# A dilated convolution on one core: four input buffers, a rearranged head, and stores on the software DMA queue

## The chip, the cores and the metric

The kernel runs on one core of a Trainium2 chip. The metric is the device time of a run in microseconds (us). A profiled execution also has a span, from its first to its last instruction, which is shorter than the measured time by 1.7 to 3.4 us in the runs of this case. Runs are sorted into fast and slow executions. The ratios below use fast ones alone; medians and ranges are over all runs, a few slow ones included. The kept profile of the kernel before is of a run classed slow (134.03 us).

## The reference

Sixteen images of 64 channels and 64x64 pixels are convolved with 128 filters of 3x3 at dilation 2, zero padded, in f32.

```python
def setup_inputs():
    batch, c_in, h, w, c_out, k, dilation = 16, 64, 64, 64, 128, 3, 2
    return {"x": randn(batch, c_in, h, w), "weight": randn(c_out, c_in, k, k) * 0.1, "dilation": dilation}

def reference(x, weight, dilation):
    # ... padding by 2 ...
    for kh in range(k):
        for kw in range(k):          # (loops over b, co, ci left out)
            output[b, co] += weight[co, ci, kh, kw] * x_pad[b, ci, kh*2:kh*2+h, kw*2:kw*2+w]
```

The input has 16.8 MB and the output 33.6 MB. Both are f32, so with 0.3 MB of weights 50.6 MB have to move whatever the kernel does.

## The kernel before

Two images form a pair: 128 partitions of 64x64 values, one load of 2.1 MB. A pair is computed in four groups of 16 output rows, so there are 32 groups. For each group ScalarE casts a chunk of the f32 pair to f16 (`cast`), VectorE adds row pairs (`rowsum`), TensorE makes three products (`psP`, `psA`, `psB`), ScalarE copies `psP` out of PSUM (`p_sb`), and VectorE adds it to `psA` and to `psB` on the way to the output buffer `osb` (`evac`). A finished pair is 4.2 MB, stored in two DMAs of 2.1 MB; only the first and the last pair are stored in halves. The instructions of each engine run in the order written. The parts that the change touches, shortened, with comments added:

```python
    LOOK = 4
    x32pool = ctx.enter_context(tc.tile_pool(name="x32pool", bufs=3))   # f32 pairs, 16 KB a partition
    xpool = ctx.enter_context(tc.tile_pool(name="xpool", bufs=3))       # f16 pairs
    opool = ctx.enter_context(tc.tile_pool(name="opool", bufs=3))       # output pairs, 32 KB a partition
    # ...
    def store(pb, m, lo, hi):
        nc.sync.dma_start(                       # loads are on nc.sync too
            out=out_img[2 * pb + m, :, lo * W : hi * W],
            in_=o_tiles[pb][:, m * HW + lo * W : m * HW + hi * W],
        )

    nc.sync.dma_start(out=w32, in_=weight.rearrange("o i h w -> o (i h w)"))
    first = [[H]] * 3
    for pb in range(min(3, npairs)):
        load(pb, first[pb])
    # ... identity; 14 warm matmuls into an "ab" PSUM tile ...
    # ... weights are combined and cast into wd ...
    cast(0)
    # ...
    rowsum(0)
    # ... wd is transposed on TensorE and copied from PSUM to w_sb by VectorE and ScalarE ...

    ahead = [1, 1]
    def prepare(n):
        n = min(n, ngroups)
        while ahead[1] < min(n - 1 if n < ngroups else n, ahead[0]):
            rowsum(ahead[1]); ahead[1] += 1
        while ahead[0] < n:
            cast(ahead[0]); ahead[0] += 1
    prepare(2)
    freed = [0]

    for G in range(ngroups):
        # ... products psP, psA, psB; copy p_sb ...
        evac(0, psA)
        prepare(min(G + 3 + G // 3, G + 1 + LOOK))
        evac(1, psB)
        if ahead[0] >= NG * (freed[0] + 1) and freed[0] + 3 < npairs:
            load(freed[0] + 3, [H])              # waits until the old pair is cast
            freed[0] += 1
        if pb in (0, npairs - 1) and g % 2 == 1:
            for m in range(2):
                store(pb, m, (g - 1) * GR, (g + 1) * GR)
        elif 0 < pb < npairs - 1 and g == NG - 1:
            for m in range(2):
                store(pb, m, 0, H)
```

Of the kernel before, what the change touches and what calls it, by code (L numbers as in the profile page):

```python
# [10 lines left out]
def kernel(  # L11
# [18 lines left out]
    nc = tc.nc  # L30

    B, CI, H, W = x.shape
# [7 lines left out]
    P = 128  # L40
    f32 = mybir.dt.float32
# [6 lines left out]
    NG = H // GR  # L48
    NBLK = GR // 4
    NH = GR // 2 * W  # L50
    npairs = B // 2
    ngroups = npairs * NG
    chunk_rows = [(g * GR + (d if g else 0), min((g + 1) * GR + d, H)) for g in range(NG)]
    LOOK = 4

    wpool = ctx.enter_context(tc.tile_pool(name="wpool", bufs=1))
    x32pool = ctx.enter_context(tc.tile_pool(name="x32pool", bufs=3))
    xpool = ctx.enter_context(tc.tile_pool(name="xpool", bufs=3))
    opool = ctx.enter_context(tc.tile_pool(name="opool", bufs=3))
    spool = ctx.enter_context(tc.tile_pool(name="spool", bufs=2))  # L60
    ppool = ctx.enter_context(tc.tile_pool(name="ppool", bufs=1, space=bass.MemoryType.PSUM))
    apool = ctx.enter_context(tc.tile_pool(name="apool", bufs=3, space=bass.MemoryType.PSUM))
# [9 lines left out]
    def load(pb, rows):  # L72

        t = x32pool.tile([P, HW], f32, tag="x32", name="x32")
        x32_tiles[pb] = t
        lo = 0
        for hi in rows:
            nc.sync.dma_start(out=t[:, lo * W : hi * W], in_=x_pair[pb, :, lo * W : hi * W])
            lo = hi

    def cast(c):
        pb, g = divmod(c, NG)
        lo, hi = chunk_rows[g]
        if g == 0:
            x16_tiles[pb] = xpool.tile([P, HW], f16, tag="x16", name="x16")
            xs_tiles[pb] = xpool.tile([P, HW // 2], f16, tag="xs", name="xs")
        nc.scalar.copy(  # L87
            out=x16_tiles[pb][:, lo * W : hi * W], in_=x32_tiles[pb][:, lo * W : hi * W]
        )

    def rowsum(c):
        pb, g = divmod(c, NG)
        v = x16_tiles[pb][:, g * GR * W : (g + 1) * GR * W].rearrange(
            "p (b e q) -> p b e q", e=2, q=2 * W
        )
        s = xs_tiles[pb][:, g * NH : (g + 1) * NH].rearrange("p (b q) -> p b q", q=2 * W)
        nc.vector.tensor_tensor(out=s, in0=v[:, :, 0], in1=v[:, :, 1], op=add)  # L97

    def store(pb, m, lo, hi):
        nc.sync.dma_start(  # L100
            out=out_img[2 * pb + m, :, lo * W : hi * W],
            in_=o_tiles[pb][:, m * HW + lo * W : m * HW + hi * W],
        )
# [3 lines left out]

    w32 = wpool.tile([CO, CI * KH * KW], f32, name="w32")
    nc.sync.dma_start(out=w32, in_=weight.rearrange("o i h w -> o (i h w)"))
    first = [[H]] * 3  # L110
    for pb in range(min(3, npairs)):
        load(pb, first[pb])

    ident = wpool.tile([P, P], f16, name="ident")
    make_identity(nc, ident)
# [1 line left out]

    warm = wpool.tile([P, 512], f16, name="warm")
    nc.vector.memset(warm, 0.0)  # L119
    wp = apool.tile([P, 1024], f32, tag="ab", name="wp")  # L120
    for i in range(14):
        nc.tensor.matmul(out=wp[:, 0:512], lhsT=warm[:, 0:P], rhs=warm)  # L122


    KINDS = 5
# [6 lines left out]
    for r in range(2):  # L132
        nc.vector.tensor_tensor(out=wdv[:, 1, :, r], in0=wv[:, 2], in1=wv[:, 1], op=sub)
        nc.scalar.copy(out=wdv[:, 4, :, r], in_=wv[:, 2])
    cast(0)
    for r in range(2):
        nc.vector.tensor_tensor(out=wdv[:, 3, :, r], in0=wv[:, 0], in1=wv[:, 1], op=sub)
    rowsum(0)
    w_sb = wpool.tile([P, KINDS * KW * CO], f16, name="w_sb")
    NT = KINDS * KW  # L140
    for q, n in ((0, 8), (8, 7)):
        wt = apool.tile([P, 1024], f32, tag="ab", name="wt")
        for t in range(q, q + n):
            nc.tensor.matmul(
                out=wt[:, (t - q) * CO : (t - q + 1) * CO],
                lhsT=wd[:, t * 2 * CI : (t + 1) * 2 * CI],
                rhs=ident,
# [5 lines left out]
    def product(ps, src, kind, blk0, nblk, first, last):  # L153

        for j in (1, 0, 2):
            dw = (j - 1) * d
            o0, o1 = max(0, -dw), W - max(0, dw)
            t = kind * KW + j
            for hb in range(2):
                pp = slice(hb * CI, (hb + 1) * CI)  # L160
                rhs = src(pp, dw + o0, dw + o1)
                po = ps[:, hb * NH + blk0 * 2 * W : hb * NH + (blk0 + nblk) * 2 * W]
                po = po.rearrange("p (r w) -> p r w", w=W)[:, :, o0:o1]
                nc.tensor.matmul(  # L164
                    out=po,
                    lhsT=w_sb[pp, t * CO : (t + 1) * CO],
                    rhs=rhs,
                    start=first and j == 1,
                    stop=last and j == 2,
                )  # L170

    def blocks(x16, b0, n, e):

        v = x16.rearrange("p (b e r w) -> p b e r w", e=2, r=2, w=W)
        return lambda pp, c0, c1: v[pp, b0 : b0 + n, e, :, c0:c1]

    ahead = [1, 1]

    def prepare(n):

        n = min(n, ngroups)
        while ahead[1] < min(n - 1 if n < ngroups else n, ahead[0]):
            rowsum(ahead[1])
            ahead[1] += 1
        while ahead[0] < n:
            cast(ahead[0])
            ahead[0] += 1

    prepare(2)
    freed = [0]  # L190

    for G in range(ngroups):
        pb, g = divmod(G, NG)
        x16 = x16_tiles[pb]
        xs = xs_tiles[pb].rearrange("p (r w) -> p r w", w=W)
        if g == 0:
            o_tiles[pb] = opool.tile([P, 2 * HW], f32, tag="osb", name="osb")
        o = o_tiles[pb].rearrange("p (m b e q) -> p m b e q", m=2, e=2, q=2 * W)
        b0 = g * NBLK

        psP = ppool.tile([P, 2 * NH], f32, tag="p", name="psP")
        sv = lambda pp, c0, c1: xs[pp, g * GR // 2 : (g + 1) * GR // 2, c0:c1]
        product(psP, sv, 0, 0, NBLK, True, True)

        psA = apool.tile([P, 2 * NH], f32, tag="ab", name="psA")
        product(psA, blocks(x16, b0, NBLK, 1), 1, 0, NBLK, True, False)
        z = 1 if g == 0 else 0
        product(psA, blocks(x16, b0 + z - 1, NBLK - z, 1), 2, z, NBLK - z, False, True)

        psB = apool.tile([P, 2 * NH], f32, tag="ab", name="psB")  # L210
        product(psB, blocks(x16, b0, NBLK, 0), 3, 0, NBLK, True, False)
        z = 1 if g == NG - 1 else 0
        product(psB, blocks(x16, b0 + 1, NBLK - z, 0), 4, 0, NBLK - z, False, True)

        p_sb = spool.tile([P, 2 * NH], f32, tag="psb", name="p_sb")
        nc.scalar.copy(out=p_sb, in_=psP)  # L216
        pv = p_sb.rearrange("p (m b q) -> p m b q", m=2, q=2 * W)

        def evac(e, ps):
            nc.vector.tensor_tensor(  # L220
                out=o[:, :, b0 : b0 + NBLK, e],
                in0=ps.rearrange("p (m b q) -> p m b q", m=2, q=2 * W),
                in1=pv,
                op=add,
            )

        evac(0, psA)
        prepare(min(G + 3 + G // 3, G + 1 + LOOK))
        evac(1, psB)

        if ahead[0] >= NG * (freed[0] + 1) and freed[0] + 3 < npairs:
            load(freed[0] + 3, [H])
            freed[0] += 1
        if pb in (0, npairs - 1) and g % 2 == 1:
            for m in range(2):
# [4 lines that stand above are left out]
# [35 lines left out]
```

## Time and profile before

| | before |
|---|---|
| measured, first three runs | 133.54 us median (132.32 to 134.15) |
| span of the profiled run | 131.3 us |
| bytes moved | 50.76 MB, mean 387 GB/s |
| rate when nothing disturbs (50 to 100 us) | 429 GB/s |
| PE busy | 107.2 us (82%) |
| end of the last evacuation | 116.6 us |

The page of the kernel before, its head. The rows with digits cut the span into 40 slices of 3.28 us; a digit is the busy share of a slice in tenths. DMA is the mean share of the 16 DMA engines and GB/s what they moved.

```profile
span 131.3 us, 2313 instructions
...
PE   6906898888999999999999999999999999900000
...
DMA  5999938999999999999999999999999999999960
GB/s 165 399 424 439 424 160 274 359 397 419 429 432 334 369 299 434 424 412 444 424 439 424 422 429 429 434 429 419 429 434 434 414 434 429 429 419 417 429 284 17
DMA packets 4185, 50.76 MB, mean 387 GB/s; under 512 B 464, under 2 KB 464, under 8 KB 592
...
```

PE looks like the bottleneck for two thirds of the span, but its row ends in zeros: TensorE is done at 115, and the DMA row goes on. 50.76 MB at 429 GB/s need 118 us, so the transfers bound the kernel, and what matters is where the GB/s row is low after the first slice: slices 5 to 8 and 12 to 14, counted from 0, that is about 16 to 30 and 39 to 49 us.

The same in stages (table by stage of the kernel before). The first numbers of a row are the stretch and its length, then the busy time of each engine with its instruction count, and the last three are the granted TensorE clock, the share of the DMA engines, and GB/s.

```profile
...
core 0: us, PE busy (x) PEld busy (x) DVE busy (x) ACT busy (x) POOL busy (x), PEclk, DMA share, GB/s
3.00:16.00 13.00, 8.61 (x56) 3.71 (x54) 5.01 (x11) 6.88 (x10) 0.00 (x0) 0.87 0.98 415
16.00:30.00 14.00, 12.05 (x112) 5.22 (x114) 9.71 (x13) 8.10 (x9) 0.00 (x0) 1.00 0.82 305
30.00:50.00 20.00, 19.54 (x190) 8.99 (x188) 17.39 (x21) 13.36 (x14) 0.00 (x0) 1.00 0.98 382
50.00:100.00 50.00, 50.00 (x488) 23.65 (x486) 43.59 (x50) 31.32 (x32) 0.00 (x0) 1.00 1.01 429
100.00:118.00 18.00, 15.22 (x150) 7.01 (x144) 13.96 (x14) 5.90 (x6) 0.00 (x0) 1.00 1.00 425
...
```

A share under 1 is time in which DMA engines held no packet (a packet is counted where it starts, so a short stretch can show a share somewhat over 1). In the trace the median 16 KB packet takes 0.611 us, and 16 engines with 16,384 bytes each in 0.611 us are exactly 429 GB/s.

What releases the transfers (timeline of the kernel before; start, duration, engine, line, operation; SPq is the queue that issues DMAs):

```profile
...
start us, us, engine line op out<-in xcount [idle before <-releaser]
...
11.08 1.43 PE L164 MATMUL psP<-xs,w_sb 64*128 64x512 f16 x6 [4.34 <-DVE w_sb L150]
...
12.30 2.38 PE L164 MATMUL psA<-x_117,w_sb 64*128 64x512 f16 x12
...
14.49 1.46 PE L164 MATMUL psB<-x_117,w_sb 64*128 64x512 f16 x12
...
19.14 0.34 SPq L78 DMA_DIRECT2D x_225<-in_x_dram  x1
...
21.32 8.44 SPq L100 DMA_DIRECT2D out_dram<-osb  x4
...
40.58 0.34 SPq L78 DMA_DIRECT2D x_476<-in_x_dram  x1
...
43.05 1.03 SPq L100 DMA_DIRECT2D out_dram<-osb  x2
...
```

The first group takes from 11.08 to 15.95. The fourth load is issued at 19.14, the first store at 21.32. The three first loads had landed by 18.6, so the DMA engines had nothing in between. The waits of the DMA queue (what it waited for, us in total, times, longest) say why:

```profile
...
SPq L100 <- DVE osb L220: 56.7, 10, 11.2
...
SPq L78 <- ACT x_117 L87: 10.3, 1, 10.3
SPq L78 <- ACT x_392 L87: 9.6, 1, 9.6
...
```

Loads (L78) wait until ScalarE has cast the pair whose buffer they take. Stores (L100) wait for VectorE's evacuation.

### The profile page before, as it was taken

The page shows a single profiled execution, that of the slowest core. Times are in us where ns is not written, and L with a number is a line of the kernel's source. Part 1 is how long each engine was busy: PE and PEld are TensorE (multiplying, and loading weights), DVE is VectorE, ACT ScalarE, POOL GpSimd, SP SyncE. Part 2 cuts the span into 40 slices and gives each one's busy share as a digit, 9 for nine tenths or more (in the row PEclk, how much of TensorE's full clock was granted, in tenths as well). Part 3 has the DMA queues.
Part 4 walks back from the last instruction along what each step waited for, and adds up shares of the span by engine and source line. Part 5 has one row for each costly group of instructions (what it writes and reads, how often), then busy time and mean ns, then how long its engine had stood idle before and what let it go on. Part 6 is the DMA issues. An engine that isn't in the chain of part 4 may idle for free.

```text
span 131.3 us, 2313 instructions
## 1 busy us (share of the span) xinstructions
PE 107.2 (82%) x989; PEld 49.3 (38%) x989; DVE 89.9 (68%) x105; ACT 66.8 (51%) x71; POOL 0.7 (1%) x6
## 2 busy tenths in 40 slices
PE   6906898888999999999999999999999999900000
PEld 2502343333445444544444444444444544400000
DVE  0704466689788888988898889888888987750000
ACT  3536555474696766665565557666766433300000
POOL 2000000000000000000000000000000000000000
PEclk9996799999999999999999999999999999998555
DMA  5999938999999999999999999999999999999960
GB/s 165 399 424 439 424 160 274 359 397 419 429 432 334 369 299 434 424 412 444 424 439 424 422 429 429 434 429 419 429 434 434 414 434 429 429 419 417 429 284 17
DMA packets 4185, 50.76 MB, mean 387 GB/s; under 512 B 464, under 2 KB 464, under 8 KB 592
## 3 DMA queue, kind: packets, MB, share of 16 engines
q1 hardware_dynamic: 4176, 50.63, 93.4%
q8 instruction: 7, 0.11, 0.3%
q14 instruction: 2, 0.02, 0.0%
HBM read 17.07 MB, written 33.55 MB: 385 GB/s over the span
## 4 chain that ended last, share of the span: by engine, by line
PE 64%; DVE 2%; DVEq 1%; ACT 1%; issue 0%
PE psA L164 26%; PE psB L164 24%; PE psP L164 14%; DVE osb L220 2%; DVEq L270 1%; ACT x_266 L87 1%; DVE xs L97 0%; DVEq L220 0%
## 5 line engine op out<-in xcount | busy, mean ns | idle before, releaser
L164 PEld LDWEIGHTS <-w_sb 64*128 64x128 f16 x960 | 46.7, 95 | 61.6 <-DVE xs L97 4.7
L216 ACT COPY p_sb<-psP 128x1024 f32<-128x1024 f32 x32 | 32.4, 1013 | 40.3 <-issue 22.1
L220 DVE TENSOR_TENSOR osb<-psA,p_sb 128x1024 f32<-128x1024 f32 x32 | 39.2, 1225 | 19.2 <-PE psA L164 18.1
L220 DVE TENSOR_TENSOR osb<-psB,p_sb 128x1024 f32<-128x1024 f32 x32 | 39.0, 1218 | 0.0
L164 PE MATMUL psP<-xs,w_sb 64*128 64x496 f16 (+1 forms) x192 | 26.2, 379 | 6.8 <-DVE w_sb L150 4.3
L164 PE MATMUL psA<-x_117,w_sb 64*128 64x496 f16 (+3 forms) x48 | 6.7, 420 | 0.0
L87 ACT CAST x_117<-x_80 128x1024 f16<-128x1024 f32 (+2 forms) x4 | 4.2, 1054 | 3.3 <-DMA x_80<-in_x_dram 3.3
L122 PE MATMUL wp<-warm 128*128 128x512 f16 x14 | 4.7, 510 | 1.2 <-DVE warm L119 1.2
L164 PE MATMUL psB<-x_117,w_sb 64*128 64x496 f16 (+3 forms) x48 | 5.6, 366 | 0.0
L164 PE MATMUL psB<-x_266,w_sb 64*128 64x496 f16 (+3 forms) x48 | 5.6, 365 | 0.0
L164 PE MATMUL psB<-x_392,w_sb 64*128 64x496 f16 (+3 forms) x48 | 5.6, 365 | 0.0
L164 PE MATMUL psB<-x_681,w_sb 64*128 64x496 f16 (+3 forms) x48 | 5.6, 365 | 0.0
L164 PE MATMUL psB<-x_844,w_sb 64*128 64x496 f16 (+3 forms) x48 | 5.6, 365 | 0.0
L164 PE MATMUL psB<-x_518,w_sb 64*128 64x496 f16 (+3 forms) x48 | 5.6, 365 | 0.0
L164 PE MATMUL psB<-x_1166,w_sb 64*128 64x496 f16 (+3 forms) x48 | 5.6, 365 | 0.0
L164 PE MATMUL psA<-x_266,w_sb 64*128 64x496 f16 (+3 forms) x48 | 5.6, 365 | 0.0
L164 PE MATMUL psA<-x_392,w_sb 64*128 64x496 f16 (+3 forms) x48 | 5.6, 365 | 0.0
L164 PE MATMUL psA<-x_681,w_sb 64*128 64x496 f16 (+3 forms) x48 | 5.6, 365 | 0.0
L164 PE MATMUL psA<-x_844,w_sb 64*128 64x496 f16 (+3 forms) x48 | 5.6, 365 | 0.0
L164 PE MATMUL psB<-x_1005,w_sb 64*128 64x496 f16 (+3 forms) x48 | 5.6, 365 | 0.0
L164 PE MATMUL psA<-x_518,w_sb 64*128 64x496 f16 (+3 forms) x48 | 5.6, 365 | 0.0
L164 PE MATMUL psA<-x_1005,w_sb 64*128 64x496 f16 (+3 forms) x48 | 5.6, 365 | 0.0
(34 smaller groups left out, 60.6 us busy)
## 6 DMA issues: line engine op xcount, KB each, us to landing
out_dram<-osb SPq DMA_DIRECT2D x12, 2048.0 KB, 16.6
out_dram<-osb SPq DMA_DIRECT2D x8, 1024.0 KB, 11.1
x_80<-in_x_dram SPq DMA_DIRECT2D x1, 2048.0 KB, 7.6
x_82<-in_x_dram SPq DMA_DIRECT2D x1, 2048.0 KB, 12.0
x_84<-in_x_dram SPq DMA_DIRECT2D x1, 2048.0 KB, 16.5
x_225<-in_x_dram SPq DMA_DIRECT2D x1, 2048.0 KB, 8.5
x_353<-in_x_dram SPq DMA_DIRECT2D x1, 2048.0 KB, 13.0
x_476<-in_x_dram SPq DMA_DIRECT2D x1, 2048.0 KB, 10.6
```

The lines of the kernel that those rows point to most:

```text
L87: nc.scalar.copy(out=x16_tiles[pb][:, lo * W : hi * W], in_=x32_tiles[pb][:, lo * W : hi * W])
L122: nc.tensor.matmul(out=wp[:, 0:512], lhsT=warm[:, 0:P], rhs=warm)
L164: nc.tensor.matmul(out=po, lhsT=w_sb[pp, t * CO : (t + 1) * CO], rhs=rhs, start=first and j == 1, stop=last and j == 2,)
L216: nc.scalar.copy(out=p_sb, in_=psP)
L220: nc.vector.tensor_tensor(out=o[:, :, b0 : b0 + NBLK, e], in0=ps.rearrange("p (m b q) -> p m b q", m=2, q=2 * W), in1=pv, op=add,)
L270: with _tile.TileContext(nc) as tc:
```

## The change

Its intent is to keep the DMA engines fed from the start to the end. The head is all that comes before the loop over the groups; warm matmuls are dummy products whose result nobody uses. A fourth f32 buffer is filled at once, without a wait; two f16 buffers remain, to make room. The head is rearranged so that the weights no longer stand behind the first cast and row sum, and a second run of warm matmuls bridges the time until the first pair arrives. Casts and row sums run further ahead. Stores go to the software DMA queue, for which GpSimd writes the descriptors (the orders that the DMA engines work through), except those of the last pair; loads stay on the hardware queue that SyncE feeds. The diff is shortened.

```diff
+    XB = 4
-    x32pool = ...(name="x32pool", bufs=3)
-    xpool = ...(name="xpool", bufs=3)
+    x32pool = ...(name="x32pool", bufs=XB)
+    xpool = ...(name="xpool", bufs=2)
@@ store
-        nc.sync.dma_start(
+        queue = nc.gpsimd if pb < npairs - 1 else nc.sync
+        queue.dma_start(
@@ fill
-    for pb in range(min(3, npairs)):
-        load(pb, first[pb])
+    for pb in range(min(XB, npairs)):
+        load(pb, [H])
@@ warm matmuls: now in the psP tile, as run_warm(14)
@@ head
-    cast(0)
     ...
-    rowsum(0)
     ... weights transposed and copied ...
+    run_warm(14)
+    ahead = [0, 0]
+    def prepare(casts, sums):
+        while ahead[0] < min(casts, ngroups):
+            cast(ahead[0]); ahead[0] += 1
+        while ahead[1] < min(sums, ngroups):
+            rowsum(ahead[1]); ahead[1] += 1
+    prepare(1, 1)
+    prepare(2, 2)
@@ loop
-        prepare(min(G + 3 + G // 3, G + 1 + LOOK))
+        prepare(min(G + 3 + (G + 1) // 2, G + 1 + LOOK), G + 3)
-        if ahead[0] >= NG * (freed[0] + 1) and freed[0] + 3 < npairs:
-            load(freed[0] + 3, [H])
+        if ahead[0] >= NG * (freed[0] + 1) and freed[0] + XB < npairs:
+            load(freed[0] + XB, [H])
```

More of the change, by code (lines that the diff above doesn't have):

```diff
@@ L53 @@
     chunk_rows = [(g * GR + (d if g else 0), min((g + 1) * GR + d, H)) for g in range(NG)]
+    XB = 4
     LOOK = 4
     wpool = ctx.enter_context(tc.tile_pool(name="wpool", bufs=1))
-    x32pool = ctx.enter_context(tc.tile_pool(name="x32pool", bufs=3))
-    xpool = ctx.enter_context(tc.tile_pool(name="xpool", bufs=3))
+    x32pool = ctx.enter_context(tc.tile_pool(name="x32pool", bufs=XB))
+    xpool = ctx.enter_context(tc.tile_pool(name="xpool", bufs=2))
     opool = ctx.enter_context(tc.tile_pool(name="opool", bufs=3))
@@ L109 @@
     nc.sync.dma_start(out=w32, in_=weight.rearrange("o i h w -> o (i h w)"))
-    first = [[H]] * 3
-    for pb in range(min(3, npairs)):
-        load(pb, first[pb])
+    for pb in range(min(XB, npairs)):
+        load(pb, [H])
     ident = wpool.tile([P, P], f16, name="ident")
@@ L119, with run_warm @@
     nc.vector.memset(warm, 0.0)
-    wp = apool.tile([P, 1024], f32, tag="ab", name="wp")
-    for i in range(14):
-        nc.tensor.matmul(out=wp[:, 0:512], lhsT=warm[:, 0:P], rhs=warm)
+    wp = ppool.tile([P, 1024], f32, tag="p", name="wp")
+    def run_warm(n):
+        for _ in range(n):
+            nc.tensor.matmul(out=wp[:, 0:512], lhsT=warm[:, 0:P], rhs=warm)
+    run_warm(14)
     KINDS = 5
@@ L175, in blocks @@
         return lambda pp, c0, c1: v[pp, b0 : b0 + n, e, :, c0:c1]
-    ahead = [1, 1]
-    def prepare(n):
-        n = min(n, ngroups)
-        while ahead[1] < min(n - 1 if n < ngroups else n, ahead[0]):
+    run_warm(14)
+    ahead = [0, 0]
+    def prepare(casts, sums):
+        while ahead[0] < min(casts, ngroups):
+            cast(ahead[0])
+            ahead[0] += 1
+        while ahead[1] < min(sums, ngroups):
             rowsum(ahead[1])
             ahead[1] += 1
-        while ahead[0] < n:
-            cast(ahead[0])
-            ahead[0] += 1
-    prepare(2)
+    prepare(1, 1)
+    prepare(2, 2)
     freed = [0]
```

## The prediction

> **What bounds the kernel now.** The transfers. The page gives 50.76 MB; undisturbed (table by stage, 60 to 100 us) the DMA engines run at share 1.01 and 429 GB/s, so the bytes alone need 118 us of the 131.3 us span. The last evacuation ends at 116.6 (timeline) and transfers go on to about 129: a backlog of 12 us. The chain of waits names PE for 64%, but PE ends at 115.2 and does not set the end.
>
> Time lies where the transfers starve. Against 429, the 3.28 us slices lose 4.0 us at 16 to 30 us (160, 274, 359, 397 GB/s) and 2.2 us at 39 to 49 us (334, 369, 299): 6.2 us. The first three loads have landed by 18.6; the fourth waits for the casts of pair 0 (issued 19.1, after a 10.3 us wait), and the first store is issued at 21.3. Loads and stores share one in-order queue: before 43 it waits up to 11 us for evacuations.
>
> **What the change does.**
> 1. A fourth f32 buffer, loaded without a wait: 2.1 MB, 4.9 us at 429 GB/s, so the fill runs to about 23.5.
> 2. Head: the weight evacuation (ends 11.5) no longer stands behind cast(0) and rowsum(0) (10.4). PE should start its first product at about 10.5 instead of 11.08. 14 more warm matmuls, at the 0.21 us of the late ones of before, take 3 us in PE's idle time (6.7 to 9.7). They keep PE warm: group 0 should take the steady 3.2 us (0.63+1.27+1.27) instead of 4.9. Groups 1 to 4 took 3.6 to 3.8 waiting for row sums, which are now one group further ahead. Compute should end about 3 us earlier, near 113.5.
> 3. Casts run ahead sooner: those of pair 0 end near 16.3, so pair 4's load is issued behind a fill that still runs; first store at about 18.3. Both starved stretches go.
> 4. Stores on the software queue: no load stands behind a store. The Trainium skill ("DMA: Bandwidth & Descriptors", "Issuing engines are not separate DMA queues") says that all queues share the same 16 engines, so the rate should stay near 429. No store of before is on this queue; its issue cost is not shown. Two f16 buffers cost no wait: the first cast of pair p+2 comes after PE's last read of pair p.
>
> **How much is on the critical path.** Nearly all of the 6.2 us, as transfers set the end. Then the backlog nearly vanishes: by my byte count the engines run dry about when pair 6 is stored (101 us), so the last store (issue 113.5, 4.9 us, ragged landing 3 us, end 1.3 us) bounds nearly as early, at 123. I take a span of 124, and 2.6 us more as measured time (134.0 against 131.3): 126.5 us. Range 124 to 131. Faster by over 2%: 0.87; within 2%: 0.10; slower: 0.03.
>
> **What would show it.** No slice under 380 GB/s between 3 and 100 us; first store issued at 18 to 19; group 0 about 3.2 us; PE's end at 112 to 113; a backlog after the last evacuation of 6 to 9 us instead of 12.
>
> **What would make it wrong.** Software descriptors that lower the rate of mixed traffic (VectorE may hold GpSimd off the shared SBUF port, as "SBUF — State Buffer" warns for some VectorE operations): 3% less rate costs 3.5 us. Or loads so far ahead that stores land late and evacuations wait for output buffers (pair 5 is tightest).

## The result, and the profile after

| | before | after |
|---|---|---|
| measured, median | 133.84 us (132.32 to 134.34, 4 runs) | 127.51 us (127.34 to 127.66, 4 runs) |
| ratio | | 0.956, 95% interval 0.948 to 0.965 |
| span of the profiled run | 131.3 us | 125.6 us |
| rate from 3 to 118 us | 404 GB/s | 423 GB/s |
| excess time of slow packets | 3.9 us | 1.6 us |
| end of the last evacuation | 116.6 us | 111.9 us |

A ratio is the mean time of one kernel's fast runs over that of the other's of the same rounds, so it is not quite the ratio of the medians. Against the median span of the fast runs of the kernel before, 130.5 us, the profiled run of the changed kernel is 4.9 us shorter; against the kept profile, which is used below, 5.7 us. The excess of slow packets is worked out from the trace: for every 16 KB packet that took over 0.64 us, the time above the usual 0.611 us, summed and divided by 16 engines. It says how much transfer time was lost while the engines were busy.

The page of the changed kernel, its head (slices of 3.14 us):

```profile
span 125.6 us, 2342 instructions
...
PE   6998999999999999999979999999999999920000
...
DMA  5999999999999999999999999999999999999970
GB/s 160 383 444 418 438 423 402 381 415 444 391 457 418 410 418 436 441 444 418 423 423 425 428 449 423 428 418 423 428 449 423 428 428 418 412 431 407 428 331 16
...
```

Between the first slice and the last two, no slice is below 381 GB/s. The same stages as before (table by stage of the changed kernel):

```profile
...
core 0: us, PE busy (x) PEld busy (x) DVE busy (x) ACT busy (x) POOL busy (x), PEclk, DMA share, GB/s
3.00:16.00 13.00, 12.66 (x94) 5.90 (x94) 7.34 (x14) 8.63 (x12) 0.00 (x0) 1.00 0.99 418
16.00:30.00 14.00, 14.00 (x138) 6.61 (x136) 12.39 (x15) 10.09 (x12) 2.25 (x4) 1.00 1.01 411
30.00:50.00 20.00, 20.00 (x200) 9.47 (x196) 17.00 (x20) 13.08 (x14) 1.31 (x3) 1.00 1.01 426
50.00:100.00 50.00, 49.27 (x480) 25.71 (x478) 42.78 (x49) 30.81 (x32) 3.96 (x8) 1.00 1.01 427
100.00:118.00 18.00, 10.51 (x102) 5.43 (x98) 10.14 (x10) 3.04 (x3) 1.06 (x2) 0.90 1.00 422
...
```

No stretch has a share under 0.99 any more, and the two low stretches went from 305 to 411 and from 382 to 426 GB/s. Against 429 over the 115 us from 3 to 118, the kernel before lost 115 x (1 - 404/429) = 6.7 us and the changed one 1.6 us. That is 5.1 of the 5.7 us of span. Of the 6.7 us, 3.9 us were slow packets; the other 2.8 us I count as idle engines.

The timeline of the changed kernel, the lines that answer to those of before (L79 are loads, L102 stores):

```profile
...
10.47 0.81 PE L167 MATMUL psP<-xs,w_sb 64*128 64x512 f16 x6 [0.34 <-DVE xs L98]
...
11.12 1.28 PE L167 MATMUL psA<-x_157,w_sb 64*128 64x512 f16 x12
...
12.23 1.43 PE L167 MATMUL psB<-x_157,w_sb 64*128 64x512 f16 x12
...
16.21 0.33 SPq L79 DMA_DIRECT2D x_245<-in_x_dram  x1
...
18.68 1.20 POOL L102 DMA_DIRECT2D out_dram<-osb  x2 [17.37 <-DVE osb L224]
...
23.55 0.33 SPq L79 DMA_DIRECT2D x_328<-in_x_dram  x1
...
25.00 1.05 POOL L102 DMA_DIRECT2D out_dram<-osb  x2 [5.13 <-DVE osb L224]
...
```

The first group now takes from 10.47 to 13.66. The fifth load is issued at 16.21, while the four first ones still run, and the first store at 18.68. One new wait appears (waits of the changed kernel):

```profile
...
DVE osb L224 <- DMA out_dram<-osb: 3.1, 2, 2.7
...
```

Pair 4 wants the output buffer of pair 1 at 61.7 us, but that store, issued at 37.9, took 26.5 us to land. VectorE stands still for 2.7 us once. The DMA share stays at 1.01 meanwhile, so no transfer starved for it; an experiment below has no such wait and is no faster.

### The profile page after: what moved, and what is told of

Its sections match the earlier page's. It is cut to its first block, busy times and chain, and to the rows that moved or that the text cites. A ratio compares the mean times of both kernels' runs of the same rounds, so it can differ in the third digit from the quotient of the medians.

```text
span 125.6 us, 2342 instructions
## 1 busy us (share of the span) xinstructions
PE 108.3 (86%) x1003; PEld 53.8 (43%) x1003; DVE 89.9 (72%) x105; ACT 66.9 (53%) x71; POOL 9.3 (7%) x22
## 4 chain that ended last, share of the span: by engine, by line
PE 54%; DMA 27%; DVE 4%; DVEq 1%; ACT 1%; issue 1%; POOL 0%; SPq 0%
PE psA L167 22%; DMA out_dram<-osb 21%; PE psB L167 21%; PE psP L167 11%; DMA x_80<-in_x_dram 6%; DVE osb L224 4%; ACT x_157 L88 1%; DVEq L274 1%; DVE xs L98 1%; POOL out_dram L102 0%; SPq L111 0%; DVEq L224 0%
## 5 line engine op out<-in xcount | busy, mean ns | idle before, releaser
L167 PEld LDWEIGHTS <-w_sb 64*128 64x128 f16 x960 | 49.9, 94 | 50.6 <-issue 1.0
L167 PE MATMUL psP<-xs,w_sb 64*128 64x496 f16 (+1 forms) x192 | 25.7, 371 | 0.3 <-DVE xs L98 0.3
L102 POOL DMA_DIRECT2D out_dram<-osb x16 | 8.6, 540 | 91.3 <-DVE osb L224 91.3
L125 PE MATMUL wp<-warm 128*128 128x512 f16 x28 | 8.3, 460 | 1.2 <-DVE warm L120 1.2
L167 PE MATMUL psB<-x_695,w_sb 64*128 64x496 f16 (+3 forms) x48 | 5.6, 365 | 0.7 <-DVE osb L224 0.7
L167 PE MATMUL psB<-x_1017,w_sb 64*128 64x496 f16 (+3 forms) x48 | 5.6, 365 | 0.0
L167 PE MATMUL psB<-x_856,w_sb 64*128 64x496 f16 (+3 forms) x48 | 5.6, 365 | 0.0
L167 PE MATMUL psB<-x_1178,w_sb 64*128 64x496 f16 (+3 forms) x48 | 5.6, 365 | 0.0
L167 PE MATMUL psA<-x_1178,w_sb 64*128 64x496 f16 (+3 forms) x48 | 5.6, 365 | 0.0
L167 PE MATMUL psA<-x_1017,w_sb 64*128 64x496 f16 (+3 forms) x48 | 5.6, 365 | 0.0
L167 PE MATMUL psA<-x_856,w_sb 64*128 64x496 f16 (+3 forms) x48 | 5.6, 365 | 0.0
L167 PE MATMUL psA<-x_695,w_sb 64*128 64x496 f16 (+3 forms) x48 | 5.6, 365 | 0.0
L167 PE MATMUL psA<-x_157,w_sb 64*128 64x496 f16 (+3 forms) x48 | 5.6, 365 | 0.0
L167 PE MATMUL psA<-x_240,w_sb 64*128 64x496 f16 (+3 forms) x48 | 5.6, 365 | 0.0
L167 PE MATMUL psA<-x_532,w_sb 64*128 64x496 f16 (+3 forms) x48 | 5.6, 365 | 0.0
L167 PE MATMUL psA<-x_369,w_sb 64*128 64x496 f16 (+3 forms) x48 | 5.6, 365 | 0.0
L167 PE MATMUL psB<-x_240,w_sb 64*128 64x496 f16 (+3 forms) x48 | 5.6, 365 | 0.0
L167 PE MATMUL psB<-x_157,w_sb 64*128 64x496 f16 (+3 forms) x48 | 5.6, 365 | 0.0
L167 PE MATMUL psB<-x_369,w_sb 64*128 64x496 f16 (+3 forms) x48 | 5.6, 365 | 0.0
```

Source lines behind the costliest of these rows:

```text
L102: queue.dma_start(out=out_img[2 * pb + m, :, lo * W : hi * W], in_=o_tiles[pb][:, m * HW + lo * W : m * HW + hi * W],)
L125: nc.tensor.matmul(out=wp[:, 0:512], lhsT=warm[:, 0:P], rhs=warm)
L167: nc.tensor.matmul(out=po, lhsT=w_sb[pp, t * CO : (t + 1) * CO], rhs=rhs, start=first and j == 1, stop=last and j == 2,)
```

## The experiments

Twelve runs were made, the first of them a repeat of the changed kernel. `before` is run beside each of them; its medians were 133.21, 132.10 and 132.80 us in the three sets, each on another chip. One of six runs of `before_head`, two of six of `after_actstores` and some of `before` (one took 154.16 us) were slow. Each run has one profile.

| run | measured us, median (range) | ratio to before | GB/s, 3 to 118 us | slow packets us |
|---|---|---|---|---|
| after_again | 127.42 (127.30 to 127.49) | 0.960 | 423 | 1.6 |
| after_hwstores | 127.83 (127.66 to 128.03) | 0.962 | 423 | 1.8 |
| before_four | 128.80 (128.33 to 129.20) | 0.970 | 412 | 2.8 |
| before_head | 128.95 (128.30 to 130.95) | 0.971 | 419 | 2.7 |
| before_sw | 133.13 (131.85 to 133.81) | 1.004 | 400 | 4.3 |
| after_nowarm2 | 127.61 (127.32 to 128.53) | 0.964 | 421 | 1.6 |
| after_actstores | 133.45 (132.79 to 135.00) | 1.003 | 402 | 1.5 |
| after_allsw | 127.99 (127.83 to 128.35) | 0.964 | 422 | 1.6 |
| transfers_seq | 123.98 (123.91 to 124.00) | 0.937 | 428 | 0.9 |
| transfers_alt | 125.88 (125.62 to 126.11) | 0.952 | 425 | 1.7 |
| transfers_alt2 | 125.69 (125.62 to 125.79) | 0.947 | 426 | 1.5 |
| transfers_two | 124.97 (124.77 to 125.13) | 0.942 | 427 | 1.2 |

### The changed kernel again

> A control: the changed kernel again, on the chip of the next three. Every theory: 127.3 to 127.7 us, span 125.6, no starved stretch before 120 us.

It came out at 127.42 us, with a span of 125.7. It is the control for the next run, which shared its chip.

### Stores back on the queue of the loads

```diff
-        queue = nc.gpsimd if pb < npairs - 1 else nc.sync
+        queue = nc.sync
```

> The changed kernel with every store back on the hardware queue that also carries the loads. Theory Q (the prediction's point 4, a load must not stand behind a store): loads are held up by stores, starved stretches come back, 129 to 131 us. Theory S (supply: each load's condition is met before the store that follows it in program order, so one queue keeps nothing waiting): no starved stretch, the rate between 30 and 110 us is the 429 of before instead of some 425, and the time is 126 to 127.5 us, equal to the control or up to 1% below it; the wait of 2.7 us for an output buffer at 61 us gets shorter or goes, because stores no longer share the engines with loads that were issued later.

127.83 us against 127.42: the ranges do not touch on this chip, so the software queue is worth 0.4 us, and no more. Theory Q falls, and with it the reason that my prediction gave in its point 4. Theory S had the right mechanism and missed the size by 0.3 us. The fifth to eighth loads are issued at about 17, 24.2, 35.6 and 48.0 us, each before the store that follows it, so nothing stands behind anything. The wait for an output buffer does not appear in the waits of this run, and the time is not better for it: that wait of 2.7 us was off the critical path. The 0.4 us fit a deeper low slice at 25 to 28 us (291 GB/s; between the first slice and the last two, the lowest of the changed kernel is 381), but one profile of each is all that this rests on.

### Only the stores moved

```diff
 def store(pb, m, lo, hi):
-        nc.sync.dma_start(
+        queue = nc.gpsimd if pb < npairs - 1 else nc.sync
+        queue.dma_start(
```

> The kernel before with only its stores moved to the software queue (last pair's excepted). Theory Q (a load standing behind a store starves the engines): both low stretches go, 128 to 130 us. Theory S (loads wait for their buffer, not for a place in the queue): the fourth load is still issued at 19 and the first store at 21, so the engines are idle from 18 to 20 as before; 132 to 134 us. A third reading, M (many packets around 18 to 27 and 41 to 49 us are slow, not missing, because loads and stores take turns in one queue): the stretch at 16 to 20 stays, the one at 39 to 49 us goes back to over 415 GB/s at a share of 1.0, and 1.5 to 2.5 us are won: 131 to 132 us.

No gain: a ratio of 1.004 with an interval of 0.997 to 1.011, so no difference clear of the noise. Theory S held. This profile is of a fast run and has both low stretches. The two rows of its table by stage that matter:

```profile
...
16.00:30.00 14.00, 12.35 (x116) 5.15 (x114) 10.28 (x12) 7.45 (x8) 1.35 (x3) 1.00 0.78 285
30.00:50.00 20.00, 19.54 (x190) 8.99 (x188) 16.87 (x21) 13.50 (x15) 1.95 (x4) 1.00 1.00 372
...
```

Idle engines at 16 to 30 (share 0.78), slow packets at 30 to 50 (share 1.00, yet 372 GB/s). Reading M expected the second stretch to be healed by separate queues, and it was not. So the slow packets of this stretch do not need loads and stores taking turns in one queue.

### Only the buffers

In short:

```diff
-x32pool bufs=3, xpool bufs=3, three first loads, load(freed + 3)
+x32pool bufs=4, xpool bufs=2, four first loads, load(freed + 4)
```

> The kernel before with only the buffers changed: four f32 pair buffers, all four filled without a wait, two f16 pair buffers; head, order of casts and stores as before. Theory B (the buffers are the cause): the fill lasts to 23.5 us and meets the load issued at 19 and the store at 21, so both starved stretches go and 5 to 6 us with them: 127.5 to 128.5 us. Theory H (the earlier head is needed as well): one of the stretches stays and the time is 129.5 to 131.5 us.

128.80 us, a gain of 3.0%, just outside what theory B gave (127.5 to 128.5) and short of theory H. The idle stretch at 18 to 20 us is gone: the share from 16 to 30 us is 1.00. But a new idle stretch appears where nobody expected one (table by stage of this run, 2 us each):

```profile
...
100.00:102.00 2.00, 2.00 (x22) 0.90 (x20) 1.52 (x3) 1.61 (x2) 0.00 (x0) 1.00 0.98 418
102.00:104.00 2.00, 2.00 (x24) 1.03 (x22) 2.00 (x3) 0.84 (x2) 0.00 (x0) 1.00 0.66 270
104.00:106.00 2.00, 2.00 (x24) 0.97 (x22) 1.85 (x4) 0.41 (x1) 0.00 (x0) 1.00 0.70 295
106.00:108.00 2.00, 2.00 (x22) 0.93 (x20) 1.51 (x3) 1.01 (x1) 0.00 (x0) 1.00 0.94 393
...
```

With the better start the DMA engines catch up with the computation, which still has the late head of before. The store of pair 6 is issued at 104.4, and the engines have little left from 102 on: by 104.6 us they have moved 42.4 MB, all that was issued before it. The kernel before had a backlog then, and its rate did not fall. From 100 to 118 us the rate is 384 GB/s here, against 425 before; against 425 that is 1.7 us.

### Only the head and the order of casts

The kernel is the changed one with `XB = 3`, three f16 buffers and all stores on `nc.sync`.

> The kernel before with only the head and the order of casts and row sums of the change: three f32 and three f16 pair buffers, all stores on the hardware queue. Theory B (the buffers are the cause): the fill still ends at 18.6 us, the first stretch shrinks but the second stays, 129.5 to 131.5 us. Theory E (either part alone feeds the engines): pair 0 is cast by 16.2, so the fourth load is issued before the fill ends and lasts to 23.5, the first store follows at 18.7; no starved stretch, 127 to 128.5 us.

128.95 us, a gain of 2.9%. Theory E has the mechanism: the share from 16 to 30 us is 1.00 with three buffers as well, because pair 0 is cast earlier, the fourth load is issued before the fill ends, and the first store follows at 18.5. The low stretch at 30 to 50 us is gone too (table by stage of this run):

```profile
...
16.00:30.00 14.00, 14.00 (x138) 7.71 (x136) 12.39 (x15) 10.16 (x11) 0.00 (x0) 1.00 1.00 372
30.00:50.00 20.00, 20.00 (x198) 11.16 (x196) 17.28 (x20) 13.01 (x14) 0.00 (x0) 1.00 1.01 426
...
```

The time is 0.5 us above its range, and the packets at 16 to 30 us are slow (372 GB/s at share 1.00, a loss of 1.9 us). One of the six runs, a slow one, took 130.95 us. The order of the head alone thus removed slow packets from 30 to 50 us (382 GB/s before, 426 here); why it does is not shown.

So each part alone gives about 3%, both together 3.8% (the version with one queue), and all three 4.0%. The parts are not summands: each of them fills the same hole at 18 to 20 us. What the second one still adds is what the first leaves open: the head, added to the buffers, gives the earlier computation that keeps the late stretch at 102 fed, and each, added to the other, leaves fewer slow packets (2.8 and 2.7 us alone, 1.8 together).

### Without the second warm matmuls

```diff
-    run_warm(14)
     ahead = [0, 0]
```

> The changed kernel without the second 14 warm matmuls. The prediction's point 2: the first group then takes 4.5 to 5 us instead of 3.2 and compute ends 1.5 us later, at about 113.5. If the transfers alone set the end, the time stays within 0.3 us of the control's 127.4, as a backlog of over 9 us is left after the last evacuation; if the head is on the critical path, 128.5 to 129.5 us.

The first group takes from 10.54 to 15.4 us, so 4.9 us instead of 3.2, and the last evacuation ends at 113.2, as expected. The median is 127.61, on another chip than the control. Six of the seven runs lie between 127.32 and 127.72. The warm matmuls do what they are for, but within the runs' scatter the time hardly depends on them. How close it is shows in the profiled run, the slowest of the seven at 128.53 (table by stage):

```profile
...
100.00:102.00 2.00, 2.00 (x24) 1.14 (x21) 1.85 (x2) 1.01 (x1) 0.58 (x2) 1.00 0.77 320
...
```

The store of pair 6 is issued at 101.4 here, 1.3 us later than in the changed kernel, and the engines had begun to run out (share 0.77).

### Stores issued from ScalarE

```diff
-        queue = nc.gpsimd if pb < npairs - 1 else nc.sync
+        queue = nc.scalar
```

> The changed kernel with all stores issued from ScalarE, a second hardware queue in place of the software queue. If the 0.4 us that the changed kernel has over its version with one queue come from having two queues, whatever their kind: 127.2 to 127.6 us, and perhaps 0.3 us better, as no software descriptors are written. If they come from the software queue itself: 127.7 to 128 us. ScalarE issues 20 stores at 0.4 to 0.5 us each and waits for evacuations before them, which may stretch some groups; with some 10 us of backlog this should not show in the time.

A clear miss: 133.45 us, the whole gain lost. ScalarE executes in order, so it stands before each store until VectorE has evacuated the pair (timeline of ScalarE in this run; ACTq is its DMA issue):

```profile
...
49.16 0.94 ACT L88 CAST x<-x 128x896 f16<-128x896 f32 x1
52.27 1.72 ACTq L102 DMA_DIRECT2D out_dram<-osb  x2
54.09 1.01 ACT L220 COPY p_sb<-psP 128x1024 f32<-128x1024 f32 x1 [3.99 <-PE psB L167]
...
```

It casts until 50.1, waits for the evacuation, issues two DMAs at 52.27, and copies `p_sb` only at 54.09. VectorE, which adds that copy, waits for it (20.7 us in nine waits over the run), and then TensorE waits for the PSUM tile. This happens at every pair, and the last evacuation ends at 121.7 instead of 111.9; between 104 and 108 us the DMA rate is 74 GB/s. I had counted on 10 us of backlog at the end. Delays at each of the eight pairs add up and use it. GpSimd has no work of its own in this loop, so it may wait as long as it likes: its 16 issues take 0.53 us each and it waits for evacuations for 91 us in total. That, more than any property of the queue, makes it a good place for the stores; SyncE, which computes nothing either, does nearly as well (after_hwstores). Whether the 0.4 us come from two queues or from the software queue, which this run was to answer, stays open: the waits of ScalarE hide it.

### All stores on the software queue

```diff
-        queue = nc.gpsimd if pb < npairs - 1 else nc.sync
+        queue = nc.gpsimd
```

> The changed kernel with the last pair's stores on the software queue as well. If the exception for the last pair is worth something, it is at the very end: a store issued from there with 0.53 us of descriptor writing and a later start, against an end that is set by a backlog of 11 us. Theory S: no difference beyond 0.3 us, 127.2 to 127.7 us. Rival (the end of a program is dearer with the software queue still at work): 127.9 to 129 us.

127.99 us (127.83 to 128.35). All six spans lie between 126.1 and 126.6, against 125.5 to 125.7 in the runs of the control, so the exception for the last pair seems to be worth 0.5 us. That is more than theory S allowed, and inside the range of the rival (127.9 to 129 us), at its low end. But the two were not measured in the same set or on the same chip, and in the profiled run of this kernel the first load landed 1.8 us later as well, so the cause is open.

### The transfers alone

Four kernels keep the loads and stores and drop the computation. They write zeros, so their results are wrong. The first has eight loads, then sixteen stores of 2.1 MB.

```python
    for pb in range(npairs):
        load(pb, [H])
    for pb in range(npairs):
        for m in range(2):
            store(pb, m, 0, H)          # from one buffer of zeros
```

> Wrong result on purpose: the same loads and stores in the same sizes without any computation, eight loads and then sixteen 2 MB stores on the hardware queue, nothing to wait for. It gives the floor of the transfers. Theory F (bytes at 429 GB/s, a start of 2 us, a ragged end and the end of the program, 4 us): span 123.5 to 125, 125.5 to 127 us measured, so the changed kernel is within 1 to 2 us of what any order can reach. Rival: the changed kernel still loses several us to dependences, then this one is under 123 us. One turn from loads to stores in the queue; theory M expects at most one stretch under 400 GB/s.

123.98 us, with a span of 122.1: the floor is lower than theory F had it and about as low as its rival wanted. The changed kernel is 3.4 us above it, of which 1.3 us are rate (423 against 428 GB/s over 115 us). Part of the rest is a ragged end: the sequential kernel has moved everything by 121 us, with 164 GB/s in the last of these microseconds, while the changed one still moves 270, 66 and 25 GB/s in the three microseconds from 121 to 124.

In the second, one load follows each pair's stores. In the third, after four loads, two loads follow back to back.

```diff
     for pb in range(4): load(pb, [H])
     ... alternating: stores of pair 0; load 4; stores of pair 1; load 5; ...
     ... alt2:        stores of pair 0; loads 4, 5; stores of pairs 1, 2; loads 6, 7; the other stores
```

> The same transfers alone, wrong result on purpose: four loads, then for each pair its two stores and one load, on one hardware queue: nine turns instead of one. Theory M (each turn between loads and stores costs about 1 us in slow packets): 6 to 9 us longer than the sequential one, with a low stretch near each turn. Rival (turns cost nothing by themselves, slow packets need something else, such as compute traffic or a queue that has run short): within 1 us of the sequential one.

> Transfers alone again, wrong result on purpose: four loads, two stores, two loads back to back, four stores, two loads, ten stores, on one hardware queue that never runs short. The alternating one showed a low stretch only at its first turn from loads to stores (20 to 24 us) and none at its later turns, which each follow one single load. Theory T (a turn is slow when all engines make it together, after at least two loads back to back): three low stretches, near 21, 41 and 71 us, and 126.5 to 128 us. Theory R (only the first turn of a program is slow; the second low stretch of the kernel before needs a queue that has run short): one low stretch, 125.5 to 126.2 us.

They took 125.88 and 125.69 us. Theory M expected nine low stretches and theory T three. Both fall, but the rival of M, within 1 us of the sequential kernel's 123.98, missed too: 1.9 us were lost, of which the first turn explains only a part. Theory R had the count and the time of the third kernel. Each run shows one, at the first turn from loads to stores (table by stage of the third kernel):

```profile
...
20.00:22.00 2.00, 0.00 (x0) 0.00 (x0) 1.00 1.06 319
22.00:24.00 2.00, 0.00 (x0) 0.00 (x0) 1.00 0.87 270
24.00:26.00 2.00, 0.00 (x0) 0.00 (x0) 1.00 1.03 442
40.00:42.00 2.00, 0.00 (x0) 0.00 (x0) 1.00 1.01 434
...
70.00:72.00 2.00, 0.00 (x0) 0.00 (x0) 1.00 1.00 426
...
```

At 20 to 24 us the share is 1.06 and 0.87 and the rate 319 and 270 GB/s; at the later turns, near 40 and 70 us, nothing happens. By its rate that first turn cost 2 x (1 - 319/429) + 2 x (1 - 270/429) = 1.3 us. The sequential kernel had its single turn at 41 us, with a rate of 319 GB/s over 2 us, so 0.5 us.

The last one puts the stores on the software queue beside the loads, as the changed kernel does.

> Transfers alone, wrong result on purpose, on the two queues of the changed kernel: all loads on the hardware queue, all stores on the software queue at once except the last pair's. If the software queue costs the engines nothing: within 1 us of the sequential one, 123.5 to 125 us, and no turn at all, so no low stretch. If mixed traffic or software descriptors lower the rate as the prediction feared: 425 GB/s or less in the mixed part and 125.5 to 127 us.

124.97 us, just inside the first range (within 1 us of the sequential one). From 16 us on it moves 429 to 432 GB/s, loads and stores mixed, so software descriptors do not lower the rate here. I had expected no low stretch at all, and there is one: from 8 to 10 us, where the first stores join the loads, it moved 270 GB/s at a share of 0.95.

## Why the prediction was right

The time was right: 126.5 us were forecast with a range of 124 to 131, and 127.51 were measured. What carried it is the sum of what the transfers lose; several of the steps below it were wrong, so part of the closeness is luck. Point by point:

- **The transfers set the end.** Right. PE is busy for 107 to 109 us in every kernel that computes, while the times run from 127.4 to 133.5 us; with the computation dropped, the transfers still need 124 us.
- **6.2 us are to be won.** Right in size: the rate from 3 to 118 us says 5.1 us, the span 5.7. Wrong in kind for a part. The prediction said that the transfers starve in both stretches. They starved at 18 to 20 us. From 30 to 50 us the share was 0.98, so about 0.4 us of 2.2 us were idle and the rest were slow packets. Over the kernel, 3.9 us of slow packets became 1.6 us.
- **The fourth buffer and the earlier head both close the hole.** Right, and the prediction listed both as if they added up. They do not: 3.0% and 2.9% alone, 3.8% together.
- **The head.** The first group took 3.2 us as forecast and began at 10.47. PE ended at 110.5, earlier than the 112 to 113 forecast, and 4.7 us earlier than before where "about 3" was said. The items that the prediction lists (0.6 us at the start, 1.7 in the first group, 0.4 to 0.6 in each of the next four) already add up to about 4. In the trace the first product came 0.6 us earlier and the first product of the sixth group 5.6 us earlier (25.86 against 31.47); some 0.9 us of this were lost again later.
- **No load stands behind a store.** True, but not a cause; this is the step of the prediction that the runs refute. One queue does the same within 0.4 us (after_hwstores), and the software queue alone gives nothing (before_sw).
- **The rate stays near 429.** Nearly: 427 from 50 to 100 us, and 423 over the whole. The 1.6 us of loss that remain are the main part of what the span exceeds my 124. The measured time is only 1.7 us above the span, where I had taken 2.6, and that error went the other way: the two errors partly cancel, which is luck.
- **The backlog nearly vanishes at pair 6, and 6 to 9 us are left at the end.** The first half is right: by 100.1 us, when the stores of pair 6 are issued, the changed kernel had moved 41.5 MB of the 42.4 MB then issued, so about 2 us of work were left. The run without warm matmuls and the one with buffers alone show the engines going short at this very place. The second half is wrong. After that point the 4.2 MB of pair 6 and the 4.2 MB of pair 7 follow in 12 us, which is faster than they drain, and transfers go on until about 124, some 12 us after the last evacuation, as many as before. I forgot to add the store of pair 6 to the last stores.
- **Pair 5 is tightest for output buffers.** It was pair 4, for 2.7 us, at no cost.
- **VectorE might hold up software descriptors.** It does not show: issues take 0.53 us, 0.67 at most, beside VectorE at 86% busy (50 to 100 us).

What stays open is why packets become slow. They do so around a run's first turn from loads to stores, even with nothing computed. The second slow stretch, at 39 to 50 us, appears in the kernel before, in before_sw and in before_four (344 GB/s from 45 to 50 us). It does not appear in before_head, in the changed kernel or in the transfers alone. Separate queues do not heal it, and two loads back to back do not make it. In the kernel before, the engines had been partly idle just ahead of it (share 0.74 from 41 to 43 us), but in before_four the share from 39 to 45 us was 1.00. None of my theories covers that. Each of these is one profile of one execution.

The changed kernel remains the fastest complete one of those that were run. A version that stores the middle pairs in halves, so that bytes come free before 100 us, was not tried.

## What to carry to other kernels

When transfers bound a kernel, read the share of the DMA engines and the bytes per second together: a low share is a missing issue, which buffers and order can mend; a low rate at full share means slow packets, which have another cause. Here a part of them went away with the order of the head as well, but no run shows why, so it cannot be planned for. Ask of each part of a change which hole it fills; two parts that fill the same one are worth little more than one, and closing an early hole can uncover a late one, where the transfers catch up with the computation. In this kernel, a DMA that has to wait for another engine belonged on the queue of an engine that has nothing else to do: on ScalarE's it cost 6 us.

## What the Trainium skill lacked or had wrong

- "DMA: Bandwidth & Descriptors", section "Where 436 GB/s comes from", says that for transfers between HBM and SBUF the HBM side binds, at about 358 GB/s per core, and in the next sentence reports 425 GB/s for a load of 16 MB. This case, with one core at work, fits the second: 427 to 429 GB/s for tens of microseconds, loads and stores mixed. It comes near the page's other ceiling, 435 GB/s.
- The same page, "Issuing engines are not separate DMA queues", is borne out as to the rate: 427 GB/s over 3 to 118 us on two queues and 428 on one with transfers alone. It says that several issuing engines save only issue time. It lacks the cost of choosing a busy one: stores issued from ScalarE made the kernel 133.45 us instead of 127.4, because ScalarE stood still before each store.
- "SBUF — State Buffer", section "SBUF: two separate sides", warns that VectorE can starve software descriptors in some of its modes. No run here shows it: 0.53 us a DMA of 2.1 MB. Whether any operation of VectorE's in this loop runs in such a mode is not shown, so the warning is not tested.
- "TensorE: Matmul & The Clock Gate", section "What's actually happening", gives a warm-up of about 3.4 us of activity, not a number of matmuls. The traces agree within 0.4 us: the first warm matmuls come every 0.43 us, and the change to 0.21 us falls at 4.2 us in the kernel before and at 5.0 us in the changed one, 3.0 and 3.8 us after the first.
- No page that I read has the slow packets: at the first turn from loads to stores the engines moved 319 and 270 GB/s over two stretches of 2 us at a share of about 1, which cost 1.3 us by the rate (transfers_alt2), and 319 GB/s over 2 us, 0.5 us, in transfers_seq.
